# Side jobs of the input projection as steps counted in products, and a re-timed down projection, in a hybrid streaming encoder layer

## The chip, the cores and the metric

The kernel runs on one core of one Trainium2 chip, as one launch. The metric is device time in microseconds (us); lower is better. A measured difference under 0.3% of the time (about 7 us here) can't be told from no change. The engines go by the names of the profile: PE is the tensor engine (matmuls) and PEld its weight loads, DVE the vector engine, ACT the scalar engine, POOL the GpSimd engine, and SP the engine that issues most DMAs.

## The reference, cut to what matters

One inference step of one encoder layer over 1024 prompt and 64 sample positions (T = 1088 columns, width 1024), everything in float32:

```
proj = rmsnorm(x) @ w_in            # z, xBC, dt, q, k, v and two gates
x   += W_out( sig(g_ssm) * (SSD scan @ W_bs) + sig(g_att) * (DiffAttn @ W_ba) )
h    = rmsnorm(x) @ w_up            # 1024 -> 2 x 2816
x   += (silu(causal_conv3(ha)) * hb) @ w_down     # 2816 -> 1024
```

q and k are normalised by head, scaled by a weight and rotated (the first 16 of 64 dimensions of a head) before attention; the rotated k is also an output. The change touches how q, k and the cached keys are finished beside the input projection, and the last product, with w_down.

## The kernel before, in words

**Precision.** Every float32 operand is split in two (`split`, L409): `hi` is a cast to the matmul's format on ACT, `lo` is the subtraction source minus hi on DVE. Three matmuls (hi·hi, hi·lo, lo·hi) make one exact enough product. The two halves of a split depend on each other: DVE's subtraction waits for ACT's cast.

**Seven products in place of eight.** The projections for q, k and z (`in_pair`, L571), the up projection (`pair`, L1475) and the down projection (`down_pair`, L1616) use a Strassen-Winograd scheme over 2 x 2 blocks. For one *pair* (two output tiles of 128 rows over all 1088 columns) there are seven products p = 0 to 6, each in two column halves s = 0, 1 of 272 columns: 14 products, each (at the usual depth of four 128-row blocks) of 12 matmuls. The *left operands* are sums and differences of weight blocks (POOL adds them, ACT and DVE split them; `left_parts`, L492). The *right parts* are sums and differences of activations, resident in SBUF as hi and lo. Each product adds to one of seven PSUM banks, and ACT (p = 0, 2) or DVE (the others) reads it out. A later product of the same bank, or the next pair, waits for that read.

**Order of work.** The program is traced in Python; a scheduler then orders each engine's instructions by program order and its own model of the time. Every engine runs its list strictly in order. `tc.issue_after(i)` pins what is traced inside it behind instruction `i` on `i`'s engine; `seen` holds the last PSUM read by ACT ("copy") and by DVE ("read") to pin behind.

**The input stage** (L809 to L828) runs 15 pairs after the first one: q and k, four pairs each, then z, eight pairs. Beside the products, at every third one (`at % 3 == 0`), one step of `beside` is taken: eight steps for the scan's step sizes (`steps`, L636), the eight blocks of cached keys (`cached_keys`, L760), and then `finishing` (L699) for q and for k: norms, twelve half rows each ("parts", L723) and four rotated quarter blocks ("turned", L735). Such a step goes through `in_turn` (L687): it *prepares* one item (POOL's DMA fetches a row into a tile `fx`, of which there are three) and *finishes* the item before: DVE scales it (L730), for k it is stored as output (L717), ACT casts hi (L410), DVE subtracts lo in place over the row (L411), and hi and lo are stored. All of a finish stands in one place of the program. Attention then loads q and k from those stores (L914).

**The way down** (L1707 to L1724). The 22 row blocks of w_down are taken in groups, `DOWN = (6, 8, 8)`; each group has four pairs (i = 0 to 11 in all), with products three blocks deep in the first group (9 matmuls) and four in the others. Each pair's results are added to the output in DRAM by POOL's accumulating DMAs. In the last up tile (f = 21) and in the last pair of a group, `right_parts` (L1593) loads the 14 right parts of the next group, each into the tile that the product just taken has freed; `right_part` (L1580) puts the split directly behind the load. The left operands of the next pair are taken one at a time after products with s = 1 (`more_left`, `down_parts`). `differences_of` (L1564) prepares differences of activations ahead.

Of the kernel before, what the change touches and what calls it, by code (L numbers as in the profile page):

```python
# [9 lines left out]
F32 = mybir.dt.float32  # L10
# [7 lines left out]
P = 128  # L18
# [43 lines left out]
IN_ROWS = dict(fs=2, fu=2, fp=3, fc=3, fx=3, ss=2)  # L62
# [27 lines left out]
def hybrid_layer(ctx: ExitStack, tc: tile.TileContext, xT, xt, prm, cst, rope, wvd, win, wbs, wba, wout, wup, wdn,  # L90
# [46 lines left out]
    wp = tc.alloc_tile_pool(name="wp", bufs=1, side="right")  # L137
    extra, turn, ahead, quick = None, 0, AHEAD_IN, QUICK

    def weight_tiles(k, m, pool=None):  # L140
        nonlocal turn
        if pool is None:
            turn = (turn + 1) % 3
        p, b = (pool, 1) if pool is not None else (extra, 1) if extra is not None and turn == 0 else (wp, 2)
        w = p.tile([P, WMAX], F32, name="w_f", tag="w_f", bufs=b)
        hi = p.tile([P, WMAX], R32, name="w_hi", tag="w_hi", bufs=b)
        lo = p.tile([P, WMAX], R32, name="w_lo", tag="w_lo", bufs=b)
        return [t[:, : k * m].rearrange("p (k m) -> p k m", k=k) for t in (w, hi, lo)]
# [231 lines left out]
    nx.release()  # L380
    extra = None
# [15 lines left out]
    for u in range(2):  # L397
        w = wp.tile([P, WMAX], F32, name="w_f", tag="w_f", bufs=2)[:, :1024]
# [93 lines left out]
    def left_parts(blocks, early=None, by=G, order=(0, 1, 2, 3)):  # L492

        a = []
        for src in blocks:
            w = wp.tile([P, WMAX], F32, name="w_f", tag="w_f", bufs=2)
# [14 lines left out]
        def shared():  # L511
            t = [wp.tile([P, WMAX], R32, name=x, tag=x, bufs=2) for x in ("w_hi", "w_lo")]
# [19 lines left out]
        hi, lo = (wp.tile([P, WMAX], R32, name=x, tag=x, bufs=2)[:, :n] for x in ("w_hi", "w_lo"))  # L532
# [154 lines left out]
    def in_turn(items):  # L687

        due = []
        for prepare, finish in chain(items, [(None, None)]):  # L690
            if prepare is not None:
                due.append((finish, prepare()))
            if len(due) > 1 or prepare is None and due:
                finish, x = due.pop(0)
                with tc.issue_after(seen["read"].ins):
                    finish(*x)
            yield

    def finishing(kind):  # L699
# [14 lines left out]
        def put(x, hi, j, n, c, w):  # L714
            rows_at = lambda y, r0: y[r0 + P * j : r0 + P * (j + n), c : c + w].rearrange("(j p) t -> p j t", p=P)
            if keep is not None:
                load(out=rows_at(keep, 0), in_=x)  # L717
            lo = x.bitcast(R32)
            split(hi, lo, x)
            for u, y in enumerate((hi, lo)):  # L720
                load(out=rows_at(to, D * u), in_=y.bitcast(F32))

        def part_of(j, c):  # L723
            def prepare():
                x = row("fx", "x")
                G.dma_start(out=x, in_=d[P * j : P * (j + 1), c : c + HT])
                return x,

            def finish(x):
                V.scalar_tensor_tensor(x, x, wcol(j), rs[:, c : c + HT], ALU.mult, ALU.mult)  # L730
                put(x.unsqueeze(1), row("fc", "xh", R32)[:, :HT].unsqueeze(1), j, 1, c, HT)

            return prepare, finish

        def turned(c):  # L735
            def prepare():
# [5 lines left out]
            def finish(x, cosine):  # L742
# [9 lines left out]
                put(x, couple(t.bitcast(R32)), 0, 2, c, QW)  # L752

            return prepare, finish

        yield from in_turn([part_of(j, c) for j in range(2, KT) for c in (0, HT)])
        for c in range(0, T, QW):
            yield from in_turn([turned(c)])

    def cached_keys():  # L760
        def part_of(j):
            def prepare():
                x = row("fx", "x")[:, :PAST]
                G.dma_start(out=x, in_=ckT[P * j : P * (j + 1), :])
                return x,

            def finish(x):
                hi = row("fc", "xh", R32)[:, :PAST]
                split(hi, x.bitcast(R32), x)
                for u, y in enumerate((hi, x)):  # L770
                    load(out=c_st[D * u + P * j : D * u + P * (j + 1), :], in_=y.bitcast(F32))

            return prepare, finish

        yield from in_turn([part_of(j) for j in range(KT)])
# [33 lines left out]
    beside = chain(steps(), cached_keys())  # L809
    for n in range(1, len(INPUT)):  # L810
        coming = in_parts(n + 1) if n + 1 < len(INPUT) else iter(())
        u = pairs[1] if n == 1 else begun_in(n)
        for at, (p, s) in enumerate(rest if n == 1 else [(p, s) for p in range(7) for s in range(2)]):
# [3 lines left out]
            if at % 3 == 0:  # L817
                next(beside, None)
# [9 lines left out]
    run(beside)  # L828
# [531 lines left out]
    def kept_weights(block, at):  # L1360

        w = wp.tile([P, WMAX], F32, name="w_f", tag="w_f", bufs=2)[:, :1024]
# [112 lines left out]
    def pair(f):  # L1475
# [31 lines left out]
        def put(h, cc):  # L1507
            for o, d, n in ((0, 0, 544),) if h == 0 else ((0, 0, 480), (480, 482, 64)):
                G.tensor_tensor(out=hb[h][:, o : o + n], in0=hb[h][:, o : o + n], in1=cc[:, d : d + n], op=ALU.mult)  # L1509
# [3 lines left out]
        for _ in range(14):  # L1513
            p, s = at
            qs = slice(QW * s, QW * (s + 1))
            if p == 0:
                S.copy(u1[:, s], pile("a", p, s, True))
            elif p == 1:
                V.tensor_tensor(out=u2[:, s], in0=pile("b", p, s, True), in1=u1[:, s], op=ALU.add)
            elif p == 2:  # L1520
                S.copy(pre[0][:, 2 + QW * s : 2 + QW * (s + 1)], pile("a", p, s, False))
# [3 lines left out]
            elif p == 3:  # L1525
                V.tensor_tensor(out=u1[:, s], in0=pile("b", p, s, False), in1=u1[:, s], op=ALU.add)
            elif p == 4:
                V.tensor_tensor(out=hb[1][:, qs], in0=pile("c", p, s, True), in1=u1[:, s], op=ALU.add)  # L1528
            elif p == 5:
                V.tensor_tensor(out=hb[0][:, qs], in0=pile("d", p, s, True), in1=u1[:, s], op=ALU.add)  # L1530
                if s == 1:
                    put(0, cc0)
            else:
                ps = pile("c", p, s, False)
                for o, d, n in ((0, 2, QW),) if s == 0 else ((0, 2 + QW, 208), (208, 484, 64)):
                    V.tensor_tensor(out=pre[1][:, d : d + n], in0=ps[:, o : o + n], in1=u2[:, s, o : o + n], op=ALU.add)
# [294 lines left out]
```

## Time and profile before

| what | us |
|---|---|
| median of three runs | 2460.97 |
| lowest and highest run | 2459.64, 2466.04 |
| the profiled execution, whole | 2462.09 |
| its span, first to last instruction | 2460.3 |
| PE busy in the span | 2399.9 |
| DVE, ACT, POOL busy in the span | 1752.4, 1223.4, 691.8 |

The span is one execution; the time around it (2462.09 less 2460.3) is launch and end. In the views, a group's row gives the busy time, the mean of one instruction in ns, and behind the second bar the idle time of that engine just before these instructions with what ended it. In a timeline row, the bracket holds the idle time before the row and its releaser. PEld, the weight load that goes with each matmul, shows gaps better than PE, whose ends are modelled.

### The profile page before, as it was taken

How to read it: one execution, taken by the hardware profiler on the slowest of the kernel's cores; microseconds unless marked ns; L12 is line 12 of the kernel's file. 1: busy time of each engine (PE TensorE's matmuls, PEld its weight loads, DVE VectorE, ACT ScalarE, POOL GpSimd, SP SyncE). 2: the span in 40 equal slices, each digit the busy share in tenths (PEclk: the TensorE clock that was granted, in tenths of full speed). 3: DMA queues.
4: the chain of work that ended last, by engine and by line, in shares of the span. 5: the costliest groups of instructions: out<-in, count | busy, mean ns of one | idle time of the engine just before them, and what ended most of it. 6: DMA issues, size and time to landing. Idle time of an engine off the chain costs nothing. (4 is left out here: it accounts for less than half of the span.)

```text
span 2460.3 us, 49370 instructions
## 1 busy us (share of the span) xinstructions
PE 2399.9 (98%) x18744; PEld 2322.8 (94%) x18744; DVE 1752.4 (71%) x3113; ACT 1223.4 (50%) x2706; POOL 691.8 (28%) x758
## 2 busy tenths in 40 slices
PE   8999999899999999999999999999999999999998
PEld 8999999899999999998899998999999999999998
DVE  4596885758687786865877665756977777787763
ACT  7354445346566565656655554434533333343441
POOL 0023233201011010114533331012254554535433
PEclk9999999999999999999999999999999999999999
DMA  7855666874554444345897954764124234268784
GB/s 254 277 169 184 224 209 215 280 211 139 164 155 139 131 146 148 108 135 190 277 329 253 332 183 149 214 204 155 55 91 172 91 123 169 80 237 232 197 216 77
DMA packets 283089, 449.79 MB, mean 183 GB/s; under 512 B 35610, under 2 KB 189347, under 8 KB 282851
## 3 DMA queue, kind: packets, MB, share of 16 engines
q1 hardware_dynamic: 271810, 420.30, 52.2%
q0 software_dynamic: 11040, 26.34, 5.5%
q8 instruction: 147, 2.41, 0.4%
q14 instruction: 92, 0.75, 0.1%
HBM read 294.03 MB, written 152.50 MB: 181 GB/s over the span
## 5 line engine op out<-in xcount | busy, mean ns | idle before, releaser
L161 PE MATMUL mm<-b,w_hi 128*128 128x272 f32 x1792 | 529.5, 296 | 3.8 <-ACT gt L847 1.9
L163 PE MATMUL mm<-b,w_lo 128*128 128x272 f32 x1792 | 523.4, 292 | 1.3 <-DVE w_lo L155 1.1
L162 PE MATMUL mm<-b,w_hi 128*128 128x272 f32 x1792 | 522.1, 291 | 0.0
L161 PEld LDWEIGHTS mm<-b,w_hi 128*128 128x128 f32 x1792 | 338.6, 189 | 9.9 <-issue 4.2
L163 PEld LDWEIGHTS mm<-b,w_lo 128*128 128x128 f32 x1792 | 338.1, 189 | 4.7 <-issue 2.2
L162 PEld LDWEIGHTS mm<-b,w_hi 128*128 128x128 f32 x1792 | 338.8, 189 | 3.2 <-issue 2.3
L876 DVE SCALAR_TENSOR_TENSOR cc<-pre,par,cc 128x272 f32<-128x272 f32 (+1 forms) x288 | 140.0, 490 | 15.7 <-ACT cc L874 12.8
L1492 PE MATMUL mx<-m,w_hi 128*128 128x272 f32 x760 | 146.5, 290 | 3.0 <-DVE hb L1528 1.8
L1492 PE MATMUL mx<-n,wh 128*128 128x272 f32 x1080 | 144.2, 288 | 1.9 <-ACT wh L479 1.0
L155 DVE TENSOR_TENSOR w_lo<-w_f,w_hi 128x1024 fp32r<-128x1024 f32 (+1 forms) x82 | 103.3, 1262 | 55.8 <-ACT w_hi L154 53.6
L864 POOL COPY pre<-pre 128x3 f32<-128x3 f32 x72 | 23.5, 327 | 417.7 <-DVE cc L878 194.7
L1492 PEld LDWEIGHTS mx<-n,wh 128*128 128x128 f32 x1080 | 138.5, 188 | 2.5 <-ACT wh L479 1.2
L479 ACT CAST w_hi<-ws 128x512 fp32r<-128x512 f32 (+1 forms) x100 | 61.0, 610 | 158.3 <-PE mx L1492 76.8
L1000 ACT ACTIVATE p_t<-sc,mx 128x512 f32<-128x512 f32 (+6 forms) x144 | 106.2, 740 | 66.4 <-DVE mx L991 32.2
L483 DVE TENSOR_TENSOR wh<-w_f,wh 128x512 fp32r<-128x512 f32 (+1 forms) x101 | 99.1, 982 | 35.1 <-ACT wh L479 35.0
L1492 PEld LDWEIGHTS mx<-m,w_hi 128*128 128x128 f32 x760 | 119.4, 188 | 4.0 <-DVE hb L1528 2.4
L154 ACT CAST w_hi<-w_f 128x1024 fp32r<-128x1024 f32 (+1 forms) x82 | 85.9, 1048 | 69.6 <-PE mm L162 46.6
L1509 POOL TENSOR_TENSOR hb<-hb,cc 128x64 f32<-128x64 f32 (+2 forms) x66 | 86.4, 1328 | 110.7 <-DVE hb L1530 52.3
L502 POOL TENSOR_TENSOR ws<-w_f 128x512 f32<-128x512 f32 (+1 forms) x46 | 61.3, 1333 | 193.9 <-DMA w_f<-in_win_dram 114.2
L479 ACT CAST wh<-w_f 128x512 fp32r<-128x512 f32 (+1 forms) x144 | 88.1, 614 | 44.8 <-POOL pre L1523 15.4
L1492 PE MATMUL mx<-m,w_lo 128*128 128x272 f32 x380 | 109.8, 289 | 0.0
L1172 ACT ACTIVATE bc<-bc,nacum 128x128 f32<-128x128 f32 (+1 forms) x288 | 87.3, 383 | 15.7 <-POOL bc L1170 15.5
(452 smaller groups left out, 6974.8 us busy)
## 6 DMA issues: line engine op xcount, KB each, us to landing
w_f<-in_win_dram SPq DMA_DIRECT2D x78, 512.0 KB, 4.3
w_f<-in_wup_dram SPq DMA_DIRECT2D x45, 512.0 KB, 3.5
bc<-a_sc SPq DMA_DIRECT2D x32, 512.0 KB, 5.8
h_sc<-hb SPq DMA_DIRECT2D x44, 272.0 KB, 2.1
ht<-h_sc SPq DMA_DIRECT2D x22, 544.0 KB, 5.2
t_sc<-ht SPq DMA_DIRECT2D x22, 544.0 KB, 3.5
out_dram<-yq POOLq DMA_DIRECT2D x44, 272.0 KB, 5.8
x_sc<-cc SPq DMA_DIRECT2D x72, 136.0 KB, 2.4
```

What stands on the lines that cost most here:

```text
L154: S.copy(hi, w)
L155: V.tensor_tensor(out=lo, in0=w, in1=hi, op=ALU.subtract)
L161: PE.matmul(ps, a_hi, b_hi, start=i == 0, stop=False)
L162: PE.matmul(ps, a_hi, b_lo, start=False, stop=False)
L163: PE.matmul(ps, a_lo, b_hi, start=False, stop=i == n - 1)
L479: S.copy(hi, src)
L483: V.tensor_tensor(out=lo, in0=src, in1=hi, op=ALU.subtract)
L876: V.scalar_tensor_tensor(cc[:, :m], pre[:, i : i + m], cw(i), cc[:, :m], ALU.mult, ALU.add)
L1000: act(p_t[:n, :nk], sc[c][:n, :nk], AF.Exp, bias=mx[:n, c : c + 1], accum_out=dst)
L1172: act(bc[:L, e, :L], bc[:L, e, :L], AF.Exp, bias=nacum[:L, ch, 8 * g + e : 8 * g + e + 1])
L1492: PE.matmul(ps, w[x][:, c], b[y][:, k], start=start and k == i == 0, stop=k == 3 and i == 2, skip_group_check=not start)
L1509: G.tensor_tensor(out=hb[h][:, o : o + n], in0=hb[h][:, o : o + n], in1=cc[:, d : d + n], op=ALU.mult)
```

## The change

Three things change; the products themselves, their number and their order inside a pair stay.

*Input stage.* `in_turn` goes. An item is now a `job`, a generator that yields the number of products until its next step: fetch; three products later the scaling (pinned behind DVE's last PSUM read) and, for k, the output store; one product later ACT's cast (pinned behind ACT's last PSUM read) and the hi store; two products later, or three for k, DVE's subtraction and the lo store. `take_turn` is called after every product, moves all running jobs on, and at every third product starts a new one. `fx` has four tiles; the room comes from a weight pool that is allocated anew with 1024 in place of 1088 columns (`wide`).

*Way down.* The groups are (8, 8, 6). Left operands are made at products written out by hand (`lefts_at`), each split pinned behind the last PSUM reads of ACT and DVE. A right part's split is no longer put behind its load: it waits in the list `landing` until at least `LANDING` = 4 products have passed, and goes out after two of every three products, pinned the same way.

*Last up tile.* The gating product (`put`) and two small copies run on DVE in place of POOL.

```diff
-DOWN = (6, 8, 8)
+DOWN = (8, 8, 6)
+LANDING = 4
-IN_ROWS = dict(fs=2, fu=2, fp=3, fc=3, fx=3, ss=2)
+IN_ROWS = dict(fs=2, fu=2, fp=3, fc=3, fx=4, ss=2)
...
+    def job(fetch, scale, hi_of, hi_rows, lo_rows, keep=None):
+        x = fetch()
+        yield 3
+        hi = lambda: None
+        if scale is not None:
+            with after("read"):
+                x = scale(x)
+            if keep is not None:
+                load(out=keep, in_=x)
+            yield 1
+        with after("copy"):
+            hi = hi_of()
+            S.copy(hi, x)
+        load(out=hi_rows, in_=hi.bitcast(F32))
+        yield 2 if keep is None else 3
+        with after("read"):
+            V.tensor_tensor(out=x.bitcast(R32), in0=x, in1=hi, op=ALU.subtract)
+        load(out=lo_rows, in_=x)
...
+    def take_turn(at):
+        for x in list(running):
+            x[0] -= 1
+            if x[0] <= 0:
+                x[0] = next(x[1], None)
+                if x[0] is None:
+                    running.remove(x)
+        if at % 3 == 0:
+            new = next(beside, False)
+            if new:
+                running.append([next(new), new])
+            return new is not False or running
...
-        yield from in_turn([part_of(j, c) for j in range(2, KT) for c in (0, HT)])
+        for j in range(2, KT):
+            for c in (0, HT):
+                yield part(j, c)
         for c in range(0, T, QW):
-            yield from in_turn([turned(c)])
+            yield turned(c)
...
-            if at % 3 == 0:
-                next(beside, None)
+            take_turn(at)
...
-    run(beside)
+    while take_turn(0):
+        for _ in range(2):
+            take_turn(1)
...
+    def landed():
+        turn[0] += 1
+        if landing and turn[0] % 3 and landing[0][0] <= turn[0]:
+            with tc.issue_after(seen["copy"].ins), tc.issue_after(seen["read"].ins):
+                split(*landing.pop(0)[1:])
...
-        split(hi, lo, raw)
+        landing.append([turn[0] + LANDING, hi, lo, raw])
...
+    def down_left(i, what):
...
+        with after("copy", "read"):
+            split(hi, lo, src)
+        left[FT + i][what] = hi, lo
...
+    def lefts_at(i, at):
+        todo = []
+        if i >= 0:
+            todo += {0: [(i, 6)]}.get(at, []) if by_token(i) else {0: [(i, 4)], 1: [(i, 5)], 3: [(i, 6)]}.get(at, [])
+        k = i + 1
+        if k < 4 * len(DOWN):
+            if by_token(i):
+                mine = {1: "load", 8: 0, 9: 1, 11: 2, 12: 3}
+            else:
+                mine = {4: "load", 8: 0, 10: 1, 11: 2, 13: 3}
+            if at in mine:
+                todo.append((k, mine[at]))
+            if by_token(k):
+                todo += {13: [(k, 5), (k, 4)]}.get(at, []) if by_token(i) else {12: [(k, 5)], 13: [(k, 4)]}.get(at, [])
+        for x in todo:
+            down_left(*x)
```

In `lefts_at`, `by_token(i)` is true for the first and the last pair of a group, whose products go through one column half and then the other; the numbers before the colons are products of pair i, those behind are left operands of pair i + 1.

More of the change, by code (lines that the diff above doesn't have):

```diff
@@ L511, in shared @@
         def shared():
-            t = [wp.tile([P, WMAX], R32, name=x, tag=x, bufs=2) for x in ("w_hi", "w_lo")]
+            t = [wp.tile([P, wide], R32, name=x, tag=x, bufs=2) for x in ("w_hi", "w_lo")]
             for i, src in enumerate((s1, q22)):
@@ L1695, in hybrid_layer @@
                 next(ahead_of)
+                landed()
             if at == 6:
@@ L1699, in hybrid_layer @@
                         differences_of(i, n)
-        while len(left[f + 1]) < 7:
+        while f + 1 < FT and len(left[f + 1]) < 7:
             more_left(f + 1)
```

175 lines of the change are left out of this document (102 added, 73 removed).

## The prediction

> **What bounds the kernel now.** I read the page's first lines, then busy time by stage, the waits of PE, and the granted clock around the longest gaps.
>
> ```profile
> span 2460.3 us, 49370 instructions
> PE 2399.9 (98%) x18744; PEld 2322.8 (94%) x18744; DVE 1752.4 (71%) x3113; ACT 1223.4 (50%) x2706; POOL 691.8 (28%) x758
> 165.00:486.00 321.00, 307.74 (x2367) 302.00 (x2366) 236.09 (x386) 149.43 (x274) 98.25 (x98) 0.99 0.66 218
> 486.00:497.00 11.00, 7.79 (x41) 7.23 (x40) 7.56 (x13) 2.90 (x4) 0.00 (x0) 0.69 0.79 245
> 2203.00:2312.00 109.00, 99.53 (x756) 96.46 (x755) 89.52 (x139) 52.89 (x91) 50.23 (x45) 0.98 0.88 249
> 2312.00:2453.00 141.00, 140.39 (x1116) 139.94 (x1115) 78.45 (x132) 44.69 (x80) 60.10 (x56) 1.00 0.68 149
> ```
>
> PE is the bound, at 98%. The number of products doesn't change, so only PE's idle time can be won, and time at a low clock. The last four rows are stretches (busy time of PE, PEld, DVE, ACT, POOL, then clock and DMA): the input stage with its side jobs, its end, the way down to its second group, and the rest. PE is idle 321.00 - 307.74 = 13.3, 11.00 - 7.79 = 3.2, 109.00 - 99.53 = 9.5 and 0.6 us, 26.6 us in all. Who ends it most, in the input stage (first row: total, times, longest) and on the way down (two):
>
> ```profile
> PE mx L584 <- DVE pre L631: 4.2, 4, 1.6
> PE mx L1650 <- ACT w_hi L479: 2.6, 1, 2.6
> PE mm L1650 <- DVE u L1655: 1.7, 1, 1.7
> ```
>
> L631 and L1655 are PSUM reads: PE waits because DVE reads its banks late. L479 casts a left operand. And the long gaps are followed by this:
>
> ```profile
> 307.29:310.70 3.41, 3.41 (x17) 3.41 (x17) 2.37 (x5) 1.27 (x4) 1.07 (x2) 0.50 0.89 272
> 481.37:484.78 3.41, 3.16 (x14) 3.16 (x15) 0.90 (x3) 2.12 (x3) 0.72 (x1) 0.50 1.01 302
> 488.19:495.02 6.83, 5.51 (x22) 5.17 (x23) 4.86 (x8) 2.22 (x3) 0.00 (x0) 0.50 0.79 252
> 2208.51:2211.93 3.42, 2.92 (x13) 2.92 (x14) 3.42 (x8) 2.38 (x5) 0.00 (x0) 0.50 1.10 376
> ```
>
> The granted clock is 0.50 there, so half of PE's busy time is lost too: 1.7 + 1.6 + 2.8 + 1.5 = 7.6 us. The change's ceiling is thus 26.6 + 7.6 = 34 us, 1.4%.
>
> The Trainium skill ("TensorE: Matmul & The Clock Gate", Part 1: The HAM clock gate) has the clock halved after about 3.4 us without work, and advises against gaps over about 3 us. The trace disagrees: gaps of 2.0 to 2.8 us (rows below) precede the four half-clock stretches. By the page, gaps as short as these would cost only themselves, and the sum below would be about 5 us smaller.
>
> **The change part by part.** *Parts of k (L730, L717, L410, L411).* A finish now stands in one place, and DVE's in-place subtraction must wait until the store of the same row has read it:
>
> ```profile
> 408.39 0.72 DVE L411 TENSOR_TENSOR x<-x,xh 128x544 fp32r<-128x544 f32 x1 [3.42 <-DMA out_dram<-x]
> L411 DVE TENSOR_TENSOR x<-x,xh 128x544 fp32r<-128x544 f32 x24 | 21.4, 894 | 14.8 <-DMA out_dram<-x 12.6 <-ACT xh L410 2.2
> 2389.32 3.00 PE mm L1650 x24
> ```
>
> DVE stands 3.42 us, and 12.6 us in all, with PSUM reads queued behind the subtraction. The third row gives the pace: 24 matmuls in 3.00 us, so a product of 12 takes 1.50 us. In this stage a bank is wanted again three products after its product ends (p = 1 before p = 3, p = 4 before p = 6), a slack of 4.5 us; 3.42 us with other work around it exceeds that. After the change the subtraction comes four products, 6 us, behind the store. That stall goes; next in line is DVE's wait for the fetched row, which comes three products ahead before and after. PE's waits between 400 and 460 us, where k's parts are finished:
>
> ```profile
> PE mx L584 <- DVE pre L631: 3.5, 3, 1.6
> PE mx L584 <- DVE u L621: 2.3, 2, 1.2
> ```
>
> 3.5 + 2.3 = 5.8 us; I keep 0.9 of it for the fetch. Gain **4.9** (bounds 0 and 5.8).
>
> *Cached keys and parts of q.*
>
> ```profile
> 213.83 0.54 POOL L764 DMA_DIRECT2D x<-in_ckT_dram  x1 [1.45 <-DMA c_st<-x]
> 217.62 0.62 ACT L410 CAST xh<-x 128x512 fp32r<-128x512 f32 x1 [5.77 <-DMA x<-in_ckT_dram]
> 305.07 0.79 DVE L730 SCALAR_TENSOR_TENSOR x<-x,wq,ss 128x544 f32<-128x544 f32 x1 [1.33 <-DMA x<-q_r]
> 306.88 1.42 PE L584 MATMUL mx<-b,wh 128*128 128x272 f32 x6 [2.03 <-ACT u L619]
> L410 ACT CAST xh<-x 128x544 fp32r<-128x544 f32 x24 | 15.5, 648 | 45.2 <-DVE x L730 39.3 <-issue 4.9 <-ACT u L619 1.0
> PE mm L584 <- ACT u L619: 1.3, 1, 1.3
> PE mx L584 <- DVE pre L631: 0.7, 1, 0.7
> ```
>
> POOL's fetch waits for a free `fx` tile until a store has landed (first row); then ACT stands at a cast for the fetched row (second) or for DVE's scaling (39.3 us in the fifth row), with its own PSUM reads behind. The last two rows are PE's other waits between 210 and 310 us. The fourth `fx` takes the first wait away, and the cast now comes one product, 1.50 us, after a scaling of 0.79. The cast of a cached key still follows its fetch by three products and can still wait. The gaps are 1.3 + 0.7 + 2.0, and 1.7 of low clock from 307.29 on, 5.7 us in all; I leave 2.2, about the first gap, half of the second and a third of the clock. Gain **3.5** (bounds 0 and 5.7).
>
> *End of the stage.* Before, an item of k in `turned` takes two steps, six products; after, one starts every three. Counted in the program, before has 8 + 9 + 2 x (4 + 3 + 13 + 8) = 73 steps at one in three products, 219 of the stage's 10 + 14 x 14 = 206, so k ends with the stage; after has 8 + 8 + 2 x (4 + 3 + 12 + 4) = 62 starts, 186 products, and the last job is through by about 190. That is 16 products, 24 us, before the stage's end.
>
> ```profile
> 481.62 0.82 PE L584 MATMUL mm<-b,w_hi 128*128 128x272 f32 x2 [2.27 <-DVE pre L631]
> 489.11 0.87 PE L986 MATMUL sc<-kh,q 128*128 128x512 f32 x2 [2.80 <-ACT w_hi L154]
> 496.85 0.37 SPq L721 DMA_DIRECT2D k_st<-x  x1
> ```
>
> The last store of k is issued at 496.85, when attention already asks for k; its loads go through SP's list behind these stores. Gaps 2.27 + 2.80 and low clock 1.6 + 2.8 are 9.5 us. The first gap goes with the rotation that blocks DVE there; the second shrinks, but attention's tiles still need memory that the last products hold. Gain **6.0** (bounds 0 and 9.5).
>
> *What is new there:* rotated blocks in flight two at a time. One costs DVE, by these groups:
>
> ```profile
> L744 DVE SCALAR_TENSOR_TENSOR x<-x,wq,ss 128x272 f32<-128x272 f32 x8 | 4.7, 621 | 0.0
> L748 DVE TENSOR_TENSOR rt<-x,rp 128x544 f32<-128x544 f32 x8 | 6.7, 840 | 4.6 <-DMA z_sc<-pre 2.4 <-DMA rp<-in_rope_dram 2.1
> L749 DVE TENSOR_TENSOR x<-x,rp 128x544 f32<-128x544 f32 x7 | 5.0, 717 | 0.1
> L750 DVE TENSOR_TENSOR x<-x,rt 128x272 f32<-128x272 f32 x7 | 4.4, 626 | 0.1
> L751 DVE TENSOR_TENSOR x<-x,rt 128x272 f32<-128x272 f32 x7 | 3.0, 431 | 0.0
> L411 DVE TENSOR_TENSOR x<-x,rt 128x544 fp32r<-128x544 f32 x7 | 6.1, 874 | 1.8 <-DMA out_dram<-x 1.2 <-ACT rt L410 0.6
> L489 DVE TENSOR_TENSOR w_lo<-ws,w_hi 128x512 fp32r<-128x512 f32 x28 | 19.2, 684 | 0.5
> L631 DVE TENSOR_TENSOR pre<-mx,u 128x272 f32<-128x272 f32 x62 | 26.5, 433 | 10.4 <-PE mx L584 10.2
> ```
>
> Two of L744 and one of each other: 2 x 0.62 + 0.84 + 0.72 + 0.63 + 0.43 + 0.87 = 4.7 us. In the same three products DVE has its share of a pair's 10 reads and 7 subtractions of left operands: 3/14 x (10 x 0.43 + 7 x 0.68) = 1.9 us. That is 6.6 us of work in 4.5. Four blocks in a row pile up 8.4 us, for q and again for k, against a slack of 4.5. In the best case nothing is late, since the means above count the overlap of neighbours twice (cost 0); in the worst 3.9 us are late both times (7.8). I take **-3.0**, nearer to none, since neither the scheduler's order nor the sum forces all of the pile before a read.
>
> *Way down.* A split behind its load makes ACT, and DVE after it, stand for the DMA:
>
> ```profile
> L410 ACT CAST ph<-ph 128x1088 fp32r<-128x1088 f32 x2 | 2.2, 1100 | 12.9 <-DMA ph<-t_sc 12.9
> L411 DVE TENSOR_TENSOR ph<-ph 128x1088 fp32r<-128x1088 f32 x2 | 2.7, 1334 | 9.3 <-ACT ph L410 9.3
> L411 DVE TENSOR_TENSOR m<-m,m 128x1088 fp32r<-128x1088 f32 x8 | 10.9, 1380 | 0.0
> L483 DVE TENSOR_TENSOR wh<-w_f,wh 128x512 fp32r<-128x512 f32 x6 | 5.0, 839 | 0.0
> ```
>
> The first two rows, 12.9 and 9.3 us, go: four products are 6 us from load to split. Left operands at fixed products end the waits on L479 and L483. What stays is DVE's load. In the last up tile it has eight right-part splits (8 x 1.38), six of left operands (6 x 0.84), ten reads (4.3), differences and gating (some 7): 27 us beside 14 products of 1.50, 21 us. Before, the same tile had all 14 splits there, each three blocks long, so it is no worse, and the deeper first group gives the next pair 21 us in place of 15.8 for the other six. `put` moved to DVE is about 1.6 us by the 0.72 of a 544-column operation, counted in the 7. Group order alone costs nothing: 9-matmul products now end the kernel, where no right parts are loaded. The stage loses 9.5 + 1.5 = 11.0; I leave 4.5, about today's first stall with its clock and some of the second. Gain **6.5** (bounds -4, if the pile-up of 6 us of the up tile falls on PE beside what remains, and 11.0).
>
> *Nothing:* the narrower weight pool holds 1024 columns, all that later loads use; its reallocation comes while earlier weights feed PE. Lost cover would cost a cast of one weight block, 1 to 2 us.
>
> **Sum.** 4.9 + 3.5 + 6.0 - 3.0 + 6.5 = 17.9 us. The span becomes 2442.4. The median lies 0.7 above the profiled span, so 2460.97 - 17.9 gives **2443 us**.
>
> **The rivals.** *More is won:* fetches land in time and the piles find room, so 27 of the 34 us come back: 2434. For it: the last 141 us of the way down lose only 0.6, with the same kind of work. Against: DVE is busy 236 of 321 us in the input stage. *It doesn't do what it says:* the stalls come from late fetches and full DMA queues (share 0.66 to 0.88), which no re-timing moves; only the keep store's wait (4.9) and a little of the way down go, some 6 us: 2455. *Slower, by one mechanism:* rotated blocks start every three products whether or not DVE keeps up. Each needs two `fc` tiles of three, so the third block's fetch of its rotation table waits, on POOL, for the first block's subtraction, and DVE then waits for that table. With 8.4 - 4.5 = 3.9 us of pile, 3 us of table wait for the third and the fourth block and 3.4 of low clock, a run of four costs 13 us, two of them 27. It decides once that exceeds the 20.9 us won elsewhere, which needs every block late: net 6 us, 2467.
>
> **How the numbers follow.** Forecast 0.52, more won 0.20, doesn't do what it says 0.16, slower 0.12. About 0.3%, 7.4 us, is what can be told from no change. The first two are faster by more than that (0.72), the third is within (0.16), the fourth slower or at its edge (0.12). The range reaches from 2429, where all but 2 us of the ceiling is won, to 2466, just short of the slower rival.
>
> **What would show it.** Right: no DVE wait on out_dram<-x at L411's successor; the last store of k some 20 us before attention's first matmul; no 0.50 clock near 307 and 482; ACT idle for right parts' DMA gone on the way down. Wrong: PE waits on L631 at the rotated blocks of q (near 340 us) or k (near 440), POOL waiting before the table's fetch, or a new gap at the last up tile longer than 2.6 us.

## The result, and the profile after

The changed kernel takes 2451.78 us (median of 6 runs, 2447.27 to 2454.38), the kernel before 2462.02 on the same chip: a ratio of 0.9956, 95% interval [0.9944, 0.9969], or 10.2 us less. Run once more on another chip (`e_again`, below) it gave 0.9962 [0.995, 0.9973]. The forecast was 2443 (17.9 us less), its range 2429 to 2466.

The profile after is of the fastest run (2447.27, 4.5 us below the median), so its differences overstate the gain: the two profiled executions stand 14.8 us apart (2462.09 and 2447.27).

The four stretches of the prediction (length; busy time of PE, PEld, DVE, ACT, POOL; clock; DMA share; GB/s), moved to where the stages now lie:

```profile
165.00:486.00 321.00, 310.57 (x2397) 305.13 (x2396) 237.86 (x400) 153.65 (x279) 101.11 (x98) 0.99 0.66 225
486.00:497.00 11.00, 11.00 (x88) 10.91 (x87) 1.37 (x11) 3.05 (x7) 0.10 (x1) 1.00 0.69 214
2190.00:2300.00 110.00, 104.81 (x796) 102.44 (x795) 85.69 (x130) 49.70 (x78) 39.30 (x33) 0.97 0.88 251
2300.00:2435.00 135.00, 134.60 (x1074) 134.38 (x1073) 88.97 (x148) 47.67 (x94) 62.88 (x60) 1.00 0.69 145
```

The number of matmuls is the same, and the end of the input stage is full. To see where in that stage the time went, the same view of four stretches of it, up to attention's start, of the kernel before:

```profile
165.00:322.00 157.00, 152.18 (x1169) 148.90 (x1168) 118.93 (x190) 69.38 (x135) 47.88 (x49) 0.99 0.60 197
322.00:366.00 44.00, 44.00 (x350) 43.91 (x349) 40.59 (x67) 19.33 (x38) 15.76 (x14) 1.00 0.66 217
366.00:476.00 110.00, 103.82 (x804) 101.67 (x803) 70.30 (x119) 56.45 (x98) 33.16 (x34) 1.00 0.73 241
476.00:498.00 22.00, 16.53 (x97) 15.75 (x96) 13.82 (x25) 7.17 (x10) 1.45 (x2) 0.77 0.86 267
```

and of the kernel after:

```profile
165.00:322.00 157.00, 153.85 (x1202) 151.38 (x1201) 121.05 (x201) 71.44 (x137) 53.17 (x52) 1.00 0.62 210
322.00:366.00 44.00, 40.84 (x290) 39.19 (x289) 29.65 (x54) 29.65 (x47) 14.52 (x12) 0.92 0.50 162
366.00:476.00 110.00, 105.87 (x829) 104.56 (x829) 82.31 (x140) 48.69 (x91) 33.43 (x34) 1.00 0.79 275
476.00:498.00 22.00, 22.00 (x175) 21.91 (x174) 6.22 (x19) 6.93 (x12) 0.10 (x1) 1.00 0.63 197
```

PE's idle time is a stretch's length less PE's busy time. It falls from 4.8 to 3.2, rises from 0 to 3.2, falls from 6.2 to 4.1, and falls from 5.5 to nothing. The second stretch, where q's rotated blocks are, was full before and is the one of the four that got worse. The half-clock stretches of after, in the same view:

```profile
341.68:348.51 6.83, 6.00 (x23) 5.40 (x24) 4.12 (x9) 5.14 (x8) 0.00 (x0) 0.50 0.71 240
2215.60:2222.42 6.82, 5.31 (x22) 4.99 (x23) 6.82 (x8) 0.90 (x3) 2.00 (x2) 0.50 0.29 43
```

The three stretches near 307, 482 and 489 us are gone; a new one of 6.83 us stands at q's rotated blocks. What ends PE's waits most now, in the input stage (first two rows, 165 to 500 us; total, times, longest) and on the way down (third, 2186 to 2300 us):

```profile
PE mx L587 <- DVE pre L634: 5.2, 4, 1.7
PE mm L587 <- DVE pre L634: 4.8, 3, 2.8
PE mm L1748 <- ACT yq L1755: 1.8, 1, 1.8
```

In the input stage nearly every wait is now for one line, L634, DVE's reads of a pair's products p = 4, 5 and 6: seven waits in some 16 pairs. Two rows of SP's queue, k's last store and attention's first fetch of k:

```profile
459.82 0.36 SPq L718 DMA_DIRECT2D k_st<-x  x1
480.50 1.11 SPq L950 DMA_DIRECT2D kh<-k_st  x2
```

From DVE's groups in the input stage (count, busy time, mean in ns, then the idle time ahead of them and what ended it):

```profile
L717 DVE TENSOR_TENSOR x<-x,xh 128x544 fp32r<-128x544 f32 (+1 forms) x32 | 32.7, 1028 | 5.8 <-DMA out_dram<-x 5.8
L717 DVE TENSOR_TENSOR x<-x,rt 128x544 fp32r<-128x544 f32 x8 | 9.4, 1183 | 1.0 <-DMA out_dram<-x 1.0
```

and from ACT's on the way down:

```profile
L413 ACT CAST m<-m 128x1088 fp32r<-128x1088 f32 x13 | 14.2, 1106 | 0.0
```

k's last store is issued 20.7 us ahead of attention's first fetch of k. The subtraction behind k's store still waits, 5.8 us in place of 12.6. ACT's casts of right parts wait for no transfer any more. One stretch got longer: the end of the kernel. These are the last matmuls of before and after:

```profile
2452.34 0.29 PE L1650 MATMUL mx<-m,w_lo 128*128 128x272 f32 x1
2435.69 0.29 PE L1748 MATMUL mx<-m,w_lo 128*128 128x272 f32 x1
```

From there to the end of the span (2460.3 and 2445.5) it is 7.7 us before and 9.5 after.

### The profile page after: what moved, and what is told of

Read it like the earlier page. It is cut to its first block, busy times and chain, and to the rows that moved or that the text cites. A ratio compares the mean times of both kernels' runs of the same rounds, so it can differ in the third digit from the quotient of the medians.

```text
span 2445.5 us, 49342 instructions
## 1 busy us (share of the span) xinstructions
PE 2394.9 (98%) x18744; PEld 2319.6 (95%) x18744; DVE 1744.6 (71%) x3118; ACT 1224.1 (50%) x2707; POOL 689.0 (28%) x753
## 4 chain that ended last, share of the span: by engine, by line
PE 66%; DMA 7%; DVE 7%; issue 3%; POOL 2%; ACT 1%; SPq 0%; POOLq 0%; DVEq 0%; ACTq 0%
PE mx L1528 9%; PE mm L162 9%; PE mm L164 9%; PE mm L163 9%; PE mm L1528 4%; PE mx L1748 4%; PE po L1071 3%; PE mx L164 2%; PE mx L162 2%; PE mx L163 2%; PE mm L1748 2%; PE mx L587 2%; PE sc L1023 2%; PE sc L1022 2%; PE pt L1051 1%
## 5 line engine op out<-in xcount | busy, mean ns | idle before, releaser
L1545 POOL TENSOR_TENSOR hb<-hb,cc 128x544 f32<-128x544 f32 (+2 forms) x63 | 81.8, 1312 | 101.8 <-DVE hb L1566 50.6
L482 ACT CAST w_hi<-ws 128x512 fp32r<-128x512 f32 x76 | 46.9, 617 | 126.5 <-PE mx L1528 75.0
L505 POOL TENSOR_TENSOR ws<-w_f 128x512 f32<-128x512 f32 x34 | 48.5, 1425 | 154.1 <-DMA w_f<-in_win_dram 64.7
L486 DVE TENSOR_TENSOR wh<-w_f,wh 128x512 fp32r<-128x512 f32 x65 | 66.7, 1028 | 26.9 <-ACT wh L482 26.9
L1430 POOL TENSOR_TENSOR s<-s,sq 128x272 f32<-128x272 f32 x24 | 30.5, 1271 | 192.9 <-DMA out_dram<-x 131.2
```

The costliest lines, as they stand in the source:

```text
L1545: (V if f + 1 == FT else G).tensor_tensor(out=hb[h][:, o : o + n], in0=hb[h][:, o : o + n], in1=cc[:, d : d + n], op=ALU.mult)
```

## The experiments

Each ratio is to runs of the kernel before on the same chip.

### The two halves apart

`e_input` keeps the input stage's part of the diff; all from the up tile's `put` on is as before, and the line below. `e_down` is the other way round.

```diff
-DOWN = (8, 8, 6)
+DOWN = (6, 8, 8)
```

> The input stage's part of the change alone (jobs counted in products, four fx tiles, the narrower weight pool); the way down is that of the kernel before. My theory: the change's 10.2 us come mostly from the end of the input stage, where the profile after gains 11 us, less 7 us lost at q's rotated blocks and plus some 3 us in the pairs of k and q: I expect 7 us less than the kernel before, 2455, with the low clock near 482 gone and a new one near 342. Rival: the stalls of the input stage only move, and the gain comes from the way down: then this kernel is within 2 us of the kernel before, 2460 to 2462.

> The way down's part alone (groups 8, 8, 6, left operands at fixed products, right parts' casts four products behind their load, the last gating on DVE); the input stage and the weight pool are those of the kernel before. My theory: the first down pair still stalls once, so it brings 3 to 5 us: 2457 to 2459, and the sum of the two halves is that of the whole change, 10 us. Rival: the way down brings the most, 8 us or more: 2454 or less.

Measured: `e_input` 0.9952 [0.9937, 0.9967], 2460.11 us against 2470.45; `e_down` 1.0003 [0.999, 1.0015], 2471.64. The whole gain is the input stage's; the way down's part adds nothing that these times can tell, within 4 us (`e_again` at 0.9962, no better than `e_input`, says the same). Both theories for the way down fell, mine (3 to 5 us) and the rival (8 or more). The profiles don't agree with the times here: in the 110 us from the first down product on, `e_input` (old way down) and then `e_down` (new) have PE busy

```profile
2192.00:2302.00 110.00, 99.52 (x748) 97.00 (x747) 90.39 (x139) 52.84 (x91) 51.77 (x45) 0.97 0.87 245
```

```profile
2214.00:2324.00 110.00, 104.39 (x790) 102.11 (x789) 85.84 (x129) 48.74 (x78) 39.24 (x33) 0.97 0.88 248
```

which is 4.9 us in favour of the new one, in one execution each. The end gives 2.2 of it back: from the last matmul to the end of the span it is 7.6 us in `e_input` and 9.8 in `e_down`. This goes with the order of the groups and nothing else: 7.6 to 7.7 us in the three profiles with 6, 8, 8 (the kernel before, `e_input`, `e_groups`), 9.5 to 9.8 in the eleven with 8, 8, 6, whichever code they run. With the short products last, POOL issues its last accumulating stores until 1.5 us after the last matmul (the kernel after), with the long ones until 0.1 us after it (before). The 2.7 us left lie within what these times can tell.

### Rotated blocks further apart, and earlier fetches

`e_spaced` is the prediction's own account of q's rotated blocks (two in flight pile up on DVE), put to the test. `e_fetch5` (second diff; parts and cached keys alone) is meant to test the waits of 3.1 to 3.4 us that DVE has for fetched rows.

```diff
-        for _ in range(4):
+        for _ in range(4 if kind == "q" else 0):
             yield
...
             yield turned(c)
+            if kind == "q":
+                yield None
```

```diff
-    def job(fetch, scale, hi_of, hi_rows, lo_rows, keep=None):
+    def job(fetch, scale, hi_of, hi_rows, lo_rows, keep=None, ahead_by=5):
...
-        yield 3
+        yield ahead_by
...
-                       None if keep is None else rows_at(keep, 0, *at))
+                       None if keep is None else rows_at(keep, 0, *at), 3)
```

> The kernel after, with q's four rotated blocks started one in six products in place of one in three; the four empty starts ahead of k's jobs are left out, so that k's jobs start where they did. My theory: the stall of 2.8 us and the 6.8 us at clock 0.50 near 342 us come from two blocks in flight that pile up on DVE; they go, and the time falls by 5 to 7 us below the kernel after, to about 2446. Rival: the stall there comes from the late table and from POOL's work beside DVE, which the spacing leaves: within 2 us of the kernel after, 2450 to 2453.

> The kernel after, with each part's fetch (and each cached key's) five products ahead of its scaling in place of three; rotated blocks stay at three. My theory: the one gap of 1.5 to 1.7 us that most pairs of the stage still have (294, 317, 391, 458 us) comes from DVE's wait of 3.1 to 3.4 us for the fetched row, so half or more of these 6 us go: 2447 to 2449. Rival one: DVE is late there for its own work, stretched beside POOL's additions, and the wait for the row only shows it: no change, 2451 to 2453. Rival two: the fx tiles are not free that early, POOL stands at its fetch with the additions for left operands behind it, and the time rises by 2 us or more.

Measured: `e_spaced` 0.9955 [0.9942, 0.9968], `e_fetch5` 0.9964 [0.9951, 0.9977]: neither is told from the kernel after. In `e_spaced` the stall near 342 shrinks from 2.8 to 1.1 us, but the next pairs' grow (at 391 and 425 us 2.4 and 1.6, where the kernel after has 1.7 and none), and PE's waits (165 to 498 us) are for the same line in the first place, 8.4 us against 10.0 of after, and 3.2 us have come at others:

```profile
PE mx L587 <- DVE pre L634: 5.6, 3, 2.4
PE mm L587 <- DVE pre L634: 2.8, 3, 1.3
```

My theory of the pile fell as it stood. That of the late rows wasn't put to the test: five products ahead didn't make the rows come sooner, since DVE's wait for k's rows is 9.3 us in the kernel after and no less in `e_fetch5`:

```profile
L760 DVE SCALAR_TENSOR_TENSOR x<-x,par,ss 128x544 f32<-128x544 f32 x12 | 13.0, 1086 | 11.2 <-DMA x<-k_r 11.2
```

What the spacing does take away is a wait that stands ahead of the stall near 342 in the kernel after, DVE's for the rotation table. POOL's fetch of that table stands 5.44 us for DVE's subtraction of an earlier block, and DVE 1.77 us for the fetch:

```profile
330.62 0.72 POOL L773 DMA_DIRECT2D rp<-in_rope_dram  x1 [5.44 <-DVE x L717]
334.73 1.33 DVE L784 TENSOR_TENSOR rt<-x,rp 128x544 f32<-128x544 f32 x1 [1.77 <-DMA rp<-in_rope_dram]
```

Between this and the late read (L634, at 342.03) three operations take 1.33, 1.81 and 1.50 us where the shortest of their kind take 0.71, 0.71 and 0.43: 2.8 us more. The stall is 2.82; `e_spaced`, whose DVE waits for the table for 0.2 us in all, keeps 1.1. So there are two causes on DVE's list here, the late table and slow operations. The other gaps that I read out in this stage have slow operations ahead of them too. POOL's timeline in `e_again`, ahead of PE's gap of 2.3 us that ends at 395.9 (start, length, engine; in brackets the idle time before):

```profile
383.99 1.59 POOL L505 TENSOR_TENSOR ws<-w_f 128x512 f32<-128x512 f32 x1 [10.84 <-DMA w_f<-in_win_dram]
385.66 1.29 POOL L506 TENSOR_TENSOR ws<-ws,w_f 128x512 f32<-128x512 f32 x1
386.90 1.79 POOL L530 TENSOR_TENSOR w_f<-w_f 128x512 f32<-128x512 f32 x1
388.64 1.09 POOL L756 DMA_DIRECT2D x<-k_r  x2
```

and rows of DVE's:

```profile
383.06 0.68 DVE L492 TENSOR_TENSOR wh<-w_f,wh 128x512 fp32r<-128x512 f32 x1
386.07 1.47 DVE L717 TENSOR_TENSOR x<-x,xh 128x544 fp32r<-128x544 f32 x1 [1.64 <-DMA out_dram<-x]
387.64 1.61 DVE L492 TENSOR_TENSOR wh<-ws,wh 128x512 fp32r<-128x512 f32 x1
393.15 0.79 DVE L760 SCALAR_TENSOR_TENSOR x<-x,par,ss 128x544 f32<-128x544 f32 x1 [3.56 <-DMA x<-k_r]
```

L492 takes 0.68 us at 383.06 and 1.61 at 387.64, L717 1.47 at 386.07, and the slow ones stand beside POOL's additions for the next pair's left operands (383.99 to 388.7). L626, which reads one operand from PSUM, keeps its length beside an addition:

```profile
437.26 1.50 POOL L530 TENSOR_TENSOR w_f<-w_f 128x512 f32<-128x512 f32 x1
437.52 0.78 DVE L626 TENSOR_TENSOR u<-mx,u 128x272 f32<-128x272 f32 x2
```

So it is over the whole stage: 20 reads with a PSUM operand ran for over half of their time beside an addition and took 0.42 to 0.44 us, as the others did; 48 operations that read SBUF only and ran beside additions took 30 us more than such operations take with no addition beside them. And the fetch of the row that DVE waits for at 393.15 stands on POOL behind those additions. So two rivals were left: the additions stretch DVE, or they hold the fetches up.

### POOL's additions left out, and moved

`e_again` is the kernel after itself. `e_noadds` (first diff) leaves the additions out in the pairs from the third on, those for p = 3 and p = 6 too; `e_addsV` (second) gives them to DVE.

```diff
+        if bare:
+            s1, s2 = q21, q12
+        else:
...
-                if p == 3:
+                if p == 3 and not bare:
...
+        if not bare:
...
-        return left_parts(blocks_of(n), early, V if n < 2 else G)
+        return left_parts(blocks_of(n), early, V if n < 2 else G, bare=n >= 2)
```

```diff
+        for _ in range(landing):
+            yield 0, None
         q11, q12, q21, q22 = a
...
-        return left_parts(blocks_of(n), early, V if n < 2 else G)
+        return left_parts(blocks_of(n), early, V, landing=0 if n < 2 else 2)
...
-            if s == 1:
+            if s == 1 or p in (3, 5):
                 more_left(n + 1)
```

> The kernel after itself, once more. The first experiments gave the input stage's part alone 0.9952 of the kernel before and the way down's part alone 1.0003, so that the halves' sum is 0.9955. If the way down brings nothing to the time, this kernel stays at 0.9955 (about 11 us); if its part is worth the 4 to 5 us that the profiles show between the first and the last down product, it comes to 0.993 to 0.994 here.

> The kernel after, with POOL's four additions a pair for the input stage's left operands left out (quadrants of the weights take the sums' places, so this leaves out part of the computation). My new theory: the one gap a pair that PE still has at L634 comes from DVE's operations with two SBUF operands, which take 1.4 to 3.1 us in place of 0.7 while POOL adds; without the additions they keep to 0.7, and PE's idle time between 165 and 498 us (10.4 us after) falls below 4 us, with no half clock near 342: 6 to 9 us less than the kernel after. Rival: the gaps come from DVE's waits for fetched rows and stores (3.1 and 3.4 us); those stay, and the time falls by 2 us or less.

> The kernel after, with the same additions on DVE in place of POOL, two steps behind the load of the weights. Theory: DVE gets 4 x 0.68 = 2.7 us more a pair and loses the doubling of some four operations, 3 to 6 us; PE's gaps fall by about half, 2 to 5 us less than the kernel after. Rival: DVE's list is longer at the place where the reads are late, or waits for the weights' load with the reads behind it: same as the kernel after, or up to 10 us slower.

Measured: `e_again` 0.9962 [0.995, 0.9973], `e_noadds` 0.989 [0.9875, 0.9906], `e_addsV` 0.992 [0.99, 0.9939]. Without the additions 18 us go (2456.76 to 2438.51), twice as much as I expected; with them on DVE 8 us (2448.56), where I expected 2 to 5. The profile of `e_addsV` is of its slowest run (2454.71; the fastest is 2439.41). The stretch from 165 to 498 us of `e_again`:

```profile
165.00:498.00 333.00, 320.55 (x2467) 314.43 (x2466) 241.62 (x416) 157.99 (x287) 102.51 (x101) 0.99 0.67 222
```

of `e_noadds`:

```profile
165.00:498.00 333.00, 331.06 (x2592) 327.20 (x2591) 216.11 (x420) 162.66 (x299) 27.08 (x46) 1.00 0.70 235
```

with two of DVE's groups in it (L764 is after's L760, L721 its L717):

```profile
L764 DVE SCALAR_TENSOR_TENSOR x<-x,par,ss 128x544 f32<-128x544 f32 x12 | 9.4, 779 | 8.9 <-DMA x<-k_r 8.9
L721 DVE TENSOR_TENSOR x<-x,rt 128x544 fp32r<-128x544 f32 x8 | 5.8, 720 | 0.2
```

and of `e_addsV`:

```profile
165.00:498.00 333.00, 325.32 (x2524) 319.94 (x2523) 244.27 (x473) 158.99 (x288) 27.61 (x47) 0.99 0.68 226
```

with the first of its four groups of additions:

```profile
L507 DVE TENSOR_TENSOR ws<-w_f 128x512 f32<-128x512 f32 x13 | 8.9, 688 | 13.1 <-DMA w_f<-in_win_dram 12.9
```

PE's idle time falls from 12.5 to 1.9 us without the additions, and L717's 1183 ns of after to 720. DVE's wait for k's fetched rows stays at 8.9 us (9.3 in the kernel after), and PE hardly feels it. So for the pairs with k's parts the stretching made the reads late, not the waits for fetches. Two things aren't separated: DVE's wait for q's rows went with the additions (4.2 us after, 0.4 here), and ACT's casts no longer wait for POOL's sums either; in `e_addsV` sums are made as before, on DVE. With the additions on DVE, 53 more of them at 0.69 us (36 us of work) make DVE's busy time only 2.7 us longer than in `e_again`: POOL's additions had cost DVE nearly as much, the 30 us above, as doing them itself. The Trainium skill ("SBUF — State Buffer", Who interferes with whom) says that a VectorE instruction with two SBUF inputs contends with a GpSimd instruction that reads SBUF, and one with at most one SBUF input, outside the two-port modes, does not. The runs agree: the operations with two SBUF operands are stretched, those with one in PSUM keep their 0.43 us.

### Group order

`e_groups` is the kernel after with the old order (first diff), `e_order` is `e_input` with the new one (second).

```diff
-DOWN = (8, 8, 6)
+DOWN = (6, 8, 8)
```

```diff
-DOWN = (6, 8, 8)
+DOWN = (8, 8, 6)
```

> The kernel after, with the groups of the way down in the order 6, 8, 8 of the kernel before. The prediction's step: the order alone costs nothing, except that a first group of 8 gives the next pair 21 us in place of 15.8 for its splits. Theory: with 6 first, the last up tile has six splits of 0.9 to 1.1 us in place of 1.4, and the first pairs are shorter: the stall of 5.5 us at the first down pair stays within 2 us of what it is, and the time within 2 us of the kernel after. Rival: the order is what takes the stalls of the second and third pair away; with 6 first they come back, and the time rises by 4 us or more.

> The input stage's part with the way down's code of the kernel before, and only the order of its groups changed to 8, 8, 6. So far, as ratios to the kernel before: old way down with 6, 8, 8 0.9952 (beside the new input stage), new way down with 8, 8, 6 0.9956 and 0.9962, new with 6, 8, 8 1.0002. My theory: the order is worth the most on the way down, since after a group of 6 the next group's quarters of 544 KB are asked for once in a product of 9 matmuls, 1.13 us, more than the DMA's 356 GB/s bring; with 8 first they have 1.50 us. With the order alone the stalls at the change from the first to the second group go and some 5 us are won on e_input: 0.993. Rival: the order helps only the new code, whose casts stand at fixed products; in the old code the waits are on left operands, and the order alone moves the time by less than 2 us or makes it slower.

Measured: `e_groups` 1.0002 [0.9989, 1.0016], beside 0.9962 of `e_again` on the same chip: 11.5 us slower, and the rival held. `e_order` 0.9963 [0.9952, 0.9975], no better than `e_input`'s 0.9952: there too the rival held, and by the times the order helps only the new code. The profiles, one execution each, don't draw that line: from the first to the last down product `e_input` takes 251.6 us and `e_order` 244.9, of which the end takes 1.9 back, so what the order is worth to the old code stays open. For the new code they agree with the times, with 258.0 us in `e_groups` and 245.5 in `e_again`. Where `e_groups` loses most, by PE's longest wait on its way down:

```profile
PE mx L1748 <- ACT wh L413: 3.9, 2, 3.5
```

the stretch in which the first group ends and the second begins:

```profile
2274.00:2292.00 18.00, 12.62 (x84) 12.08 (x83) 15.44 (x20) 12.21 (x17) 10.27 (x8) 0.81 1.12 356
```

and ACT's casts of right parts there:

```profile
L413 ACT CAST n<-n 128x1088 fp32r<-128x1088 f32 x4 | 4.4, 1102 | 4.3 <-DMA n<-t_sc 3.4 <-DMA n<-h_sc 0.9
```

The same change of groups in `e_again`, from 8 to 8:

```profile
2282.00:2310.00 28.00, 27.92 (x219) 27.36 (x218) 25.14 (x33) 18.10 (x26) 9.51 (x8) 1.00 1.11 329
```

In a group's last pair one quarter of the next group is loaded per product: 128 x 1088 x 4 = 557 KB for a group of 8. After a group of 6 a product has 9 matmuls, 1.13 us, which asks for 495 GB/s; the queues bring 356, ACT stands 4.3 us at casts whose data isn't there, and the left operands' casts, now at fixed places behind them, come late for PE (3.5 us). After a group of 8 a product is 1.50 us and asks for 371 GB/s, and PE loses 0.1 us.

### What the findings add up to

On top of `e_addsV`: q's rotated blocks one in six products (`e_addsV_sp`, the edit of `e_spaced`); the way down's four additions a pair on DVE, three of them ahead of the pair's first cast (`e_addsV_dn`, the diff); both (`e_best`).

```diff
-            G.tensor_tensor(out=s1, in0=q21, in1=q22, op=ALU.add)
...
+        if what == 0:
...
+            with after("read"):
+                V.tensor_tensor(out=s1, in0=q21, in1=q22, op=ALU.add)
```

> The additions for the input stage's left operands on DVE as in e_addsV (0.992 of the kernel before), and q's rotated blocks one in six products as in e_spaced. Theory: what is left near 342 us (a gap of 2.3 us and 3.4 us of half clock) is DVE's own pile of two rotated blocks; with both, it goes: 3 to 4 us less than e_addsV, 0.9905. Rival: the spacing only shifts the load, as in e_spaced, which stood no better than the kernel after: 0.992 again.

> e_addsV with the way down's additions for left operands on DVE too, right ahead of the first cast of a pair. Theory: DVE's splits of right parts, which take 2.1 to 2.5 us beside POOL in place of 1.28, keep to 1.28; the stalls of the first down pair shrink by 1 to 3 us: 0.991. Rival: DVE is full between 2195 and 2222 us as it is, and 2.7 us more a pair cost PE 2 to 5 us: 0.993 to 0.994.

> The three edits together: the additions for left operands on DVE in the input stage and on the way down, and q's rotated blocks one in six products. They act in different stretches or on different causes, so if each is worth what its profile shows (the input stage from 165 to 498 us with less than 4 us of idle PE time, the first down pair without the stall of 1.8 to 2.2 us), the ratio to the kernel before is 0.990, about 24 us less. Rival: the spacing and the move on the way down are within the noise of e_addsV's 0.992, and together bring nothing more: 0.991 to 0.992.

Measured: 0.991 [0.9894, 0.9925], 0.9913 [0.9898, 0.9927] and, for `e_best`, 0.9904 [0.9888, 0.9921]: 2444.26 us against 2468.58, 24 us less than the kernel before and faster than the kernel after. Between the three and `e_addsV` the times don't decide, and the profiles don't either. At q's rotated blocks (322 to 366 us) PE is idle for 3.2 us in `e_addsV`, for nothing in `e_addsV_sp` (busy 43.97 of 44.00), but for 0.3 us in `e_addsV_dn` too, which has the input stage of `e_addsV`, without the spacing:

```profile
322.00:366.00 44.00, 40.76 (x298) 39.12 (x297) 32.86 (x67) 28.34 (x46) 2.51 (x4) 0.96 0.56 172
322.00:366.00 44.00, 43.73 (x339) 42.82 (x338) 32.88 (x66) 32.79 (x50) 3.58 (x6) 1.00 0.52 163
```

The difference between these two executions of the same input stage is the rotation table: ahead of its stall of 2.3 us `e_addsV` has

```profile
341.75 0.73 DVE L786 TENSOR_TENSOR rt<-x,rp 128x544 f32<-128x544 f32 x1 [3.77 <-DMA rp<-in_rope_dram]
```

and the read that PE waits for right behind it, while `e_addsV_dn` waits for tables for 0.3 us in all. The spacing takes the table's wait out of the way (0.0 us in `e_addsV_sp` at these blocks); how often it is there without the spacing isn't known. The whole stage in `e_best`:

```profile
165.00:498.00 333.00, 331.06 (x2595) 327.42 (x2594) 246.75 (x477) 160.01 (x290) 27.60 (x47) 1.00 0.69 234
```

PE is idle for 1.9 us of it, as in `e_noadds`, with all sums made; in `e_addsV_dn` for 3.1.

## Why the prediction was right, and where it was off

The sign, the range and the mechanism of the largest term were right; the size was too large by 7.7 us. By its number alone the result can't be told from the rival at 2455: 2451.78 is 3.2 us from that and 8.8 from the forecast. What speaks for the forecast is where the gain came from. Its terms against the profile after (idle PE time, and half of PE's busy time at a low clock: 1.7 and 4.4 us of before from the prediction's rows, 6.00/2 and 5.31/2 of after; 11.6 for the way down before is 9.5 + 0.6 + 1.5; the end of the kernel is 7.7 before and 9.5 after):

| step | predicted | in the profile |
|---|---|---|
| parts of k (366 to 476) | 4.9 | 6.2 - 4.1 = 2.1 |
| cached keys, parts of q (165 to 322) | 3.5 | 4.8 + 1.7 - 3.2 = 3.3 |
| rotated blocks (322 to 366) | -3.0 | 0 - 3.2 - 3.0 = -6.2 |
| end of the stage (476 to 498) | 6.0 | 5.5 + 4.4 - 0 = 9.9 |
| way down | 6.5 | 11.6 - 5.2 - 0.4 - 2.7 + 7.7 - 9.5 = 1.5 |
| sum | 17.9 | 10.6, of the 14.8 between the two executions |

The other 4.2 us lie outside these stretches. That the input stage's four terms come near what `e_input` measured (11.4 forecast, 10.3 measured) is in part luck: rotated blocks lost 3.2 us more than forecast and parts of k gave 2.8 less, and the end of the stage gave 3.9 more. The low clock's share in these terms is partly chance as well: whether a gap brings it depends on where the gap falls (last section).

- **End of the stage:** the count of starts held. k's jobs end 20.7 us ahead of attention's first fetch of k, against "16 products, 24 us, before the stage's end" of the working. I left 3.5 us for attention's tiles that "still need memory that the last products hold"; nothing was late there, and the gain passed the bound of 9.5 by a little. It alone is about as large as the whole measured gain.
- **Parts of k:** "That stall goes" was half true. The subtraction stands four products behind the store, and still waits 5.8 of the 12.6 us.
- **Cached keys and parts of q:** as sized.
- **Rotated blocks:** the step that failed in kind. The place was named, and PE's wait there, like POOL's wait ahead of the table's fetch, was listed as what would show it wrong; both came. The working's durations were means of 0.84 and 0.87 us, which mix two sorts: 0.72 alone, and 1.5 and more beside POOL's additions. I took the excess for a count of overlaps that could only help. `e_noadds` shows that the additions make the reads late. The other part of the stall is the wait for the rotation table, 1.77 us of 2.82 in the kernel after and all of it in `e_addsV`. A pile of blocks by itself is shown by no run.
- **Way down:** the waits named went (ACT's for right parts, the stall of 2.6 us at L479), and a stall of 1.8 us with 6.8 us of half clock came at the last up tile, inside the bound. But the longer end takes 1.8 us back, and the times show nothing of the 1.5 left: `e_down` stands at 1.0003, and whether a gain of up to 3 us is there stays open. "Group order alone costs nothing" was wrong twice. The sentence behind it, "9-matmul products now end the kernel", names the place of the 1.8 us and puts it at nothing. And beside the new code the old order costs the whole gain: without it the change would be worth nothing (`e_groups`, 1.0002). The step looked at the kernel's last group, not at the rate at which a group of 6 asks for the quarters of a group of 8.
- **The narrower pool, for nothing:** no run took it apart; nothing in the traces points to it.
- **The rivals:** "It doesn't do what it says" at 2455 named the late fetches as what no re-timing moves. The fetch waits for k's rows did stay, but they weren't the cause (`e_noadds`). The slower rival's mechanism is there, fetch, subtraction and table as it says (2.8 us of waits after, at L784), and it makes the stall at q's rotated blocks together with the additions; it is too small to turn the sign.

## What to carry to other kernels

A mean duration of a group that is well above its shortest members is a lead: look at what runs on the other engines during the long ones before planning with the mean. Work given to an idle engine isn't free when it makes the full engine's instructions longer; here 53 small additions cost DVE nearly as much on POOL (30 us) as on DVE itself (36). And a schedule with fixed places carries the transfer rate that it asks for: count the bytes per product at each change of group before choosing the order.

## What the runs showed of the hardware

DVE operations of 512 and 544 columns with two SBUF operands took 0.67 to 0.79 us alone and mostly 1.1 to 1.8 beside POOL additions, at most 3.4 (`e_again`, 165 to 498 us); the additions themselves took 1.27 to 1.31 alone and up to 1.8 beside such operations; DVE operations of 272 columns with a PSUM operand kept 0.42 to 0.44. A short gap can bring a half clock, and a longer one none. In `e_addsV_sp` a gap of 1.66 us was enough:

```profile
499.11:502.52 3.41, 1.75 (x11) 1.38 (x10) 2.35 (x5) 3.41 (x11) 0.00 (x0) 1.00 0.63 162
502.52:505.93 3.41, 3.41 (x16) 3.27 (x16) 3.06 (x8) 2.75 (x7) 0.00 (x0) 0.50 0.42 122
```

In the kernel after, a gap of 2.35 us at the stage's start was followed by full speed:

```profile
123.80 0.52 PE L587 MATMUL mx<-b,w_hi 128*128 128x272 f32 x2 [2.35 <-ACT u L622]
119.82:123.23 3.41, 1.64 (x13) 1.41 (x12) 0.00 (x0) 0.00 (x0) 0.00 (x0) 1.00 1.03 357
123.23:126.64 3.41, 2.84 (x22) 2.84 (x23) 2.73 (x5) 2.65 (x7) 1.30 (x2) 1.00 1.13 358
```

The traces show what decides. In each of the 14 profiles the half-clock stretches begin on a grid of 3.41 us, whose place differs from run to run; the rows above lie on it. Cut along that grid from 60 us on, 70 stretches at full clock were followed by one at half clock, and PE had been idle for 1.45 us or more in each of them; in the 9559 that were followed by full clock it had been idle for 1.77 us at most. The gap of 1.66 us falls into one stretch, that of 2.35 into two, 1.77 and 0.57. So a gap of about half a stretch can cost a half clock, and where it falls on the grid is chance.

The gap near 124 us is 0.84 us in the profile of the kernel before and 2.35 to 3.9 in all later ones; `e_down`, which has the old input stage, has it too (2.61 us), so the input stage's change didn't make it.
